# A hybrid mLSTM and attention step on one core: samples' output rows on 128 partitions, output weights loaded inside the heads' output product, third K tile's sums moved

## The chip, the cores and the metric

The kernel runs on one core of one Trainium2 chip. The core has a matrix engine (TensorE, PE in the profile, with its weight loads as PEld), a vector engine (VectorE, DVE), a scalar engine (ScalarE, ACT), GpSimd (POOL) and a queue engine (SyncE, SP) that issues nearly all transfers. Each engine works through its own instructions in order; semaphores make one wait for another. The metric is the device time of one execution in microseconds; lower is better.

## The reference, cut to what matters

One layer over 1024 prompt tokens and 32 sample tokens (8 sequences of 4), width 1024, all in float32: an mLSTM branch and a windowed attention branch, merged by gates, then an output product and two residual and norm steps.

```python
y_m, C, n, m = mlstm_branch(mq, mk, mv, mi, mf, mo, mz, C0, n0, m0, b_i, b_f, g_mn)
y_a = o.astype(x.dtype) * jax.nn.silu(az)
u = jax.nn.sigmoid(gm) * (y_m @ w_mo) + jax.nn.sigmoid(ga) * (y_a @ w_ao)
x = x + gate * (u @ w_o)            # gate: one row for the prompt, one per sample sequence
y = rmsnorm(x, g_final)             # for the prompt and for the samples
```

The change is in the last two lines: `u @ w_o` (called w_out in the kernel), the residual and the norm, for 1024 prompt rows and 32 sample rows.

## The kernel before

The large products are float32. Each operand is split into a high and a low part (`wh`/`wl`, `h`/`l`), and three matmuls (high by high, high by low, low by high) make one product. Products of 2 by 2 blocks are done with seven products instead of four times two, from sums and differences of the blocks; the names b11, b21, b22, t1 to t4 are the seven operands on the weights' side.

The work comes in this order: norm and conditioning of the tokens; gates and heads with their states (pairs of products 0 to 13 in `pairs`: heads, gates, two query gates, four head gates), with the attention units and the samples' work beside them; the attention's output product (tiles ax, ay, az, aw); the heads' output product `w_mo` (eight pieces d = 0 to 7, tile g_w_mo, whose sums tgw_mo complete `u`); and then the row stage, which is where most of the change lies.

*The row stage.* The prompt's rows are done as four row pairs i = 0 to 3 (`blocks_of_rows`), 2 by 128 rows each. A pair takes seven products of 128 by 512, each of four K tiles (KA = 0, 1, 4, 5) by three matmuls, so twelve matmuls. They run in the order 1, 5, 6, 2, 7, 3, 4 (in the last pair 3 before 7), into PSUM tiles that the profile calls foX (products 1 and 2), foZ (5), foW (6 and 3, on a copy of foX) and foY (7 and 4, on a copy of foW). Their weights are, in that order, b11, t1, t2, b21, t3, b22, t4. The row operands u0 to u3 are split two or three products ahead by `row_start()`: a cast to the high part on ScalarE (u0wh), the low part by a subtraction on VectorE (u0wl). Where a sum is needed first it is formed on VectorE, as `us` for product 5. After the products come adds to the residual x_prompt (tiles rows_l and rows_h), squares on ScalarE, the norm's small chain (fss, fv, fy, fw) and the scaled output y_p.

*The samples' rows.* The 32 sample rows stand in a group of small products (tile fo), four products at a time, one for each 32-column strip of the array: 32 rows by 512 columns, with K tiles kq to kq+3 in the four strips. Four such groups cover the two halves of the columns and the two halves of K. They stand after product 6 and after product 3 in rows 0 and 1. Their weights are plain w_out, loaded into four tiles (misc 1 and 7, parts of rows_l and rows_h) that each group reuses. The four strips are summed afterwards on VectorE (tile fo8s) with 32 partitions.

*The output weights.* The prompt's weights are w_out times the gate, in seven sums per K tile, each split in two (wosh, wosl). They are formed by `out_weights()` beside the heads. Tiles 0, 1 and 4 are stored to DRAM (woD) and loaded again by `weights_out(n)` after each piece d of the w_mo product; tile 5 stays in SBUF. The third tile (4) begins at the head gates and waits until the samples of all heads are done.

*What sets the order.* TensorE's order is the order in which the code is written; a planner (`Side`) hands out the side work by estimated TensorE time (`side.now`), and each `yield` names a lag until the next step. In the row stage VectorE and ScalarE follow the code as well; before it the scheduler may move their instructions. SP issues transfers in one queue; a transfer that must wait for its buffer holds up all that are behind it.

## Time and profile before

| what | value |
|---|---|
| median of 3 runs | 841.75 us (840.94 to 841.95) |
| the profiled execution's own time | 841.93 us |
| its span | 840.1 us |
| TensorE busy | 808.5 us, 96% |
| VectorE busy | 605.7 us, 72% |
| ScalarE busy | 417.8 us, 50% |
| mean bandwidth | 197 GB/s |

The profile is of one execution. In a timeline's row stand start, duration, engine, source line, operation, tiles written and read, form and count, and in brackets the idle time before it and what ended it. Most work has line 220, 261 or 275, those of the helpers, so tiles tell the place. An idle engine matters only where the engine that sets the end waits for it.

### The profile page before, as it was taken

The numbers are of one execution on the slowest core, as the hardware profiler recorded it, in microseconds if no ns is written. First come the engines' busy times: TensorE is split into PE (matmuls) and PEld (weight loads), VectorE is DVE, ScalarE is ACT, GpSimd is POOL, SyncE is SP. The second block draws the span as 40 slices with busy tenths as digits, with TensorE's granted clock in tenths as the row PEclk, the third lists the DMA queues.
The fourth block names the chain that finished last, engine by engine and source line by source line (L and its number), as shares of the span: only waits on it lengthen the run. The fifth ranks groups of instructions, "written<-read, shape, count | busy, mean of one in ns | idle before, by whom it ended". The sixth has DMA issues, their size and how long they took to land. (4 is left out here: it accounts for less than half of the span.)

```text
span 840.1 us, 15038 instructions
## 1 busy us (share of the span) xinstructions
PE 808.5 (96%) x5105; PEld 665.6 (79%) x5105; DVE 605.7 (72%) x1503; ACT 417.8 (50%) x1019; POOL 46.4 (6%) x111
## 2 busy tenths in 40 slices
PE   6999999999999999999999999999999999959996
PEld 3779797888788788888888888888886789937775
DVE  4889886646656546577576977897879977844887
ACT  5664365655465564556557554444456541124332
POOL 0120000000000001000001010000014010000000
PEclk9999999999999999999999999999999999989999
DMA  9994667446445324637737744646384899274422
GB/s 336 365 318 154 221 192 224 140 160 207 155 131 181 129 88 157 225 90 275 250 117 219 255 153 153 199 145 201 137 290 164 260 372 369 65 270 150 157 101 107
DMA packets 113025, 165.49 MB, mean 197 GB/s; under 512 B 21152, under 2 KB 55072, under 8 KB 112916
## 3 DMA queue, kind: packets, MB, share of 16 engines
q1 hardware_dynamic: 107300, 153.78, 55.5%
q10 hardware_dynamic: 4176, 6.56, 2.1%
q0 software_dynamic: 1472, 4.20, 1.3%
q8 instruction: 40, 0.66, 0.3%
q14 instruction: 37, 0.30, 0.1%
HBM read 115.51 MB, written 50.00 MB: 197 GB/s over the span
## 5 line engine op out<-in xcount | busy, mean ns | idle before, releaser
L220 ACT ACTIVATE p<-p,nmx 128x256 f32<-128x256 f32 (+1 forms) x64 | 31.0, 486 | 18.7 <-DVE nmx L220 18.3
L275 PE MATMUL g_aq<-h_h,wh_aq 128*128 128x384 f32 (+1 forms) x96 | 32.2, 336 | 0.0
L275 PE MATMUL g_aq<-h_h,wl_aq 128*128 128x384 f32 (+1 forms) x96 | 30.9, 322 | 0.0
L275 PE MATMUL g_aq<-h_l,wh_aq 128*128 128x384 f32 (+1 forms) x96 | 30.8, 321 | 0.0
L275 PE MATMUL g_w_mo<-ym_l,wh_w_mo 128*128 128x384 f32 (+1 forms) x96 | 30.8, 321 | 0.0
L275 PE MATMUL g_w_mo<-ym_h,wh_w_mo 128*128 128x384 f32 (+1 forms) x96 | 30.8, 321 | 0.0
L275 PE MATMUL g_w_mo<-ym_l,wl_w_mo 128*128 128x384 f32 (+1 forms) x96 | 30.8, 321 | 0.0
L220 DVE CUSTOM_DVE_ANT_0 p<-sc,cst,sink 128x256 f32<-128x256 f32 (+1 forms) x64 | 26.1, 463 | 5.3 <-PE sc L275 5.2
L220 ACT CAST wosh<-wor 128x512 fp32r<-128x512 f32 x24 | 14.9, 620 | 16.8 <-DVE wor L220 16.8
L275 PEld LDWEIGHTS g_aq<-h_h,wh_aq 128*128 128x128 f32 x96 | 18.0, 188 | 2.6 <-issue 1.5
L220 DVE TENSOR_TENSOR et<-et,S 128x384 f32<-128x384 f32 (+1 forms) x12 | 6.1, 509 | 19.1 <-PE S L275 16.4
L220 DVE SCALAR_TENSOR_TENSOR tgw_mo<-tgw_mo,g_w_mo 128x384 f32<-128x384 f32 (+1 forms) x24 | 12.4, 518 | 10.2 <-PE g_w_mo L275 9.6
L261 POOL DMA_DIRECT2D oD<-uqv x16 | 8.8, 552 | 184.3 <-ACT uqv L220 164.6
L275 PE MATMUL sc<-ukv,uqv 64*128 64x256 f32 (+1 forms) x128 | 18.0, 390 | 0.7 <-DMA ukv<-kD 0.7
L220 DVE TENSOR_TENSOR wosl<-wor,wosh 128x512 fp32r<-128x512 f32 x24 | 16.4, 685 | 2.8 <-ACT wosh L220 2.7
L275 PEld LDWEIGHTS g_w_mo<-ym_l,wh_w_mo 128*128 128x128 f32 x96 | 18.0, 188 | 0.0
L275 PEld LDWEIGHTS g_w_mo<-ym_h,wh_w_mo 128*128 128x128 f32 x96 | 18.0, 188 | 0.0
L275 PEld LDWEIGHTS g_aq<-h_l,wh_aq 128*128 128x128 f32 x96 | 18.0, 188 | 0.0
L275 PEld LDWEIGHTS g_w_mo<-ym_l,wl_w_mo 128*128 128x128 f32 x96 | 18.0, 188 | 0.0
L275 PEld LDWEIGHTS g_aq<-h_h,wl_aq 128*128 128x128 f32 x96 | 18.0, 188 | 0.0
L220 DVE COPY p<-pt 128x512 f32<-128x512 f32 (+1 forms) x16 | 10.5, 654 | 10.3 <-PE pt L280 10.3
L220 ACT ACTIVATE sq<-rows_h 128x512 f32<-128x512 f32 (+2 forms) x14 | 8.1, 579 | 19.0 <-issue 14.4
(2057 smaller groups left out, 2830.6 us busy)
## 6 DMA issues: line engine op xcount, KB each, us to landing
x<-xT SPq DMA_DIRECT2D x16, 256.0 KB
early_h<-w_ada SPq DMA_DIRECT2D x8, 512.0 KB
adar_ga<-w_ada SPq DMA_DIRECT2D x16, 256.0 KB
wr_ga<-w SPq DMA_DIRECT2D x16, 256.0 KB
wr_gm<-w SPq DMA_DIRECT2D x16, 256.0 KB
taD<-gt SPq DMA_DIRECT2D x16, 256.0 KB
tmD<-gt SPq DMA_DIRECT2D x16, 256.0 KB
wor<-w_out SPq DMA_DIRECT2D x16, 256.0 KB
```

Source lines behind the costliest of these rows:

```text
L220: ins = f(*args, **kw)
L261: ins = (eng or nc.sync).dma_start(out, in_)
L275: in_order(nc.tensor.matmul(out, lhsT, rhs, start=start, stop=stop, skip_group_check=more))
```

## The change

1. *Samples on 128 partitions.* The four strips now hold the four blocks of 256 output columns, 32 rows each, instead of four K tiles. A group is eight products of 32 by 256 (two K tiles) and the strips need no sum afterwards: gate, residual, square and scaling work on tiles of 128 by 256 (gs8, x8, y8, gf8). The squares of the four strips are added by four one-column products (fo8s) ahead of product 5 in the last row. The groups stand after product 3 in row 0, after 6 and 3 in row 1, and after 6 in row 2. The layouts of x_sample, y_s and of gsD (the samples' gates in DRAM) follow.
2. *Loads.* Two output weights each more are asked for after d = 5 to 7, and the rest in row 0, after the first w_out loads and x_prompt in the code; gsD, g_final (now once for the prompt, and in four pieces for the samples) and x_sample follow them in the code.
3. *Third K tile.* Its sums begin at product 5 of pair 11 and no longer wait for the samples; its lag is 2.2.
4. *Row order.* In rows 0 to 2 the adds of products 7 and 3 stand before the next split. Rows 4 and 5 of the output blocks are multiplied by g_final on VectorE first and then scaled on ScalarE.

```diff
@@ out_weights
-                    lag = 3.0
+                    lag = 2.2 if k == KA[2] else 3.0
-                while k == KA[2] and len(samples_done) < NH + 1:
-                    yield 0.5, ""
@@ hook
-            if n == len(pairs) - NH + 1 and not begun:
+            if (n, i) == (11, 5):
                 begun.append(4)
@@ heads' output product
-            weights_out((3, 3, 3, 2, 2, 1, 0, 0)[d])
-        weights_out(len(wo_parts))
+            weights_out((3, 3, 3, 2, 2, 2, 1, 1)[d])
...
-        gsb, gf = misc[0], misc[2]
-        dma(gf, a["g_final"].to_broadcast((128, D)), True)
-        S.activation(gf, gf, AF.Copy, scale=-1.0)
-        dma(gsb[:NS], gsD, True)
+        gf = misc[2]
+        gs8, gf8, x8, y8 = (misc[0][:, c:c + 256] for c in range(0, D, 256))
...
+        def weighted(xb, c):
+            V.tensor_tensor(xb[:, c], xb[:, c], gf[:, c], op=ALU.mult)
@@ sample_rows
+            def load(q):
+                for n, t in enumerate(raws):
+                    k = 2 * q + n // 2
+                    dma(t, a["w_out"][k * 128:(k + 1) * 128, HALF[n % 2]], q == 0)
+
+            def products(q):
+                for n in range(8):
+                    k, j = 2 * q + n // 4, n % 4
+                    mm(acc[32 * j:32 * j + 32], u(k, SEQ, NS), raws[n // 2][:, 256 * (j % 2):256 * (j % 2) + 256], start=(k == 0), stop=(k == KT - 1), share=4)
...
-                for j in (32, 64, 96):
-                    V.tensor_tensor(sums[f], acc[f][j:j + 32], sums[f], op=ALU.add)
-                V.tensor_tensor(sums[f], sums[f], gsb[:NS, HALF[f]], op=ALU.mult)
+            V.tensor_tensor(gs8, acc, gs8, op=ALU.mult)
+            V.tensor_tensor(x8, x8, gs8, op=ALU.add)
+            square(x8, sq8)
@@ rows
         rows8 = sample_rows()
+        next(rows8)
...
-            aside(0)
+            if not i:
+                weights_out(len(wo_parts))
+                dma(gs8, gsD)
+                dma(gf, a["g_final"].to_broadcast((128, D)))
+                S.activation(gf, gf, AF.Copy, scale=-1.0)
+                for j in range(4):
+                    dma(gf8[32 * j:32 * j + 32], a["g_final"][:, 256 * j:256 * j + 256].to_broadcast((32, 256)))
+                S.activation(gf8, gf8, AF.Copy, scale=-1.0)
+                dma(x8, a["x_sample"])
...
+            if i == 3:
+                sum8 = pb([128, 512], "fo8s")[:, :1]
+                for j in range(4):
+                    mm(sum8[32 * j:32 * j + 32], cst[:, C_S32:C_S32 + 32], sq8, start=True, stop=True, share=4)
...
-            aside(0, 1, 2)
+            aside(1, 2)
             for c in range(2) if i else ():
-                rows_out(2 * i - 2 + c, before[0][c], rs[:, c:c + 1])
+                rows_out(2 * i - 2 + c, before[0][c], rs[:, c:c + 1], V if nxt else None)
...
             if nxt:
+                seventh()
                 row_start()
-                seventh()
                 square(xb[1][:, hi], ss[:, 3:4])
+                first_row()
                 row_start()
-                first_row()
                 aside(0, 1, 2)
```

What stands where on the engines follows from the code and the scheduler. The first place is SP's queue up to the first w_out loads. Before, from the last t4 weights on (ahead of them stand the last tgw_mo from tmD and the other ten weights of t3, b22 and t4):

```order
L261 DMA wo_t4h<-woDt41h 128x512
L261 DMA wo_t4l<-woDt41l 128x512
L261 DMA wo_t4h<-woDt44h 128x512
L261 DMA wo_t4l<-woDt44l 128x512
L261 DMA rows_l_8763<-g_final 128x1024
L261 DMA rows_l_8763<-gsD 32x1024 x2
L261 DMA rows_l_8763<-x_prompt 128x1024
L261 DMA rows_h_8764<-x_prompt 128x1024
L261 DMA rows_l_8763<-w_out 128x512 x2
L261 DMA rows_h_8764<-w_out 128x512 x2
```

After, from the last tgw_mo on:

```order
L261 DMA tgw_mo_2_8613<-tmD_166 128x288
L261 DMA rows_l_8747<-gsD 128x256
L261 DMA rows_l_8747<-g_final 128x1024
L261 DMA wo_b22h<-woDb220h 128x512
L261 DMA wo_b22l<-woDb220l 128x512
L261 DMA rows_l_8747<-g_final 32x256 x4
L261 DMA rows_l_8747<-x_sample 128x256
L261 DMA wo_b22h<-woDb221h 128x512
L261 DMA wo_b22l<-woDb221l 128x512
L261 DMA rows_l_8747<-w_out 128x512 x2
L261 DMA rows_h_8748<-w_out 128x512 x2
L261 DMA rows_l_8747<-x_prompt 128x1024
```

The w_out loads moved ahead of x_prompt and of the last b22 and all t4 weights; gsD is now the first transfer behind tgw_mo, and x_prompt with those eight weights follows w_out.

The second place is VectorE at the end of the w_mo product, from the sum of its next to last part up to `us`, the operand of product 5 in row 0 (wosl, wor: the last K tile's weights). Before:

```order
L220 TENSOR_TENSOR wor_8204<-wor_8204,wor_8200 128x512
L220 SCALAR_TENSOR_TENSOR tgw_mo_1_8607<-tgw_mo_1_8607,g_w_mo_8705 128x384
L220 SCALAR_TENSOR_TENSOR tgw_mo_2_8609<-tgw_mo_2_8609,g_w_mo_8720 128x288
L220 TENSOR_TENSOR wosl<-wor_8204,wosh 128x512
L220 TENSOR_TENSOR us<-u_h_7686,u_l_7687 128x512
L220 TENSOR_TENSOR u_l_7687<-u_l_7687,tgw_mo_1_8607 128x384
```

After:

```order
L220 SCALAR_TENSOR_TENSOR tgw_mo_1_8611<-tgw_mo_1_8611,g_w_mo_8713 128x384
L220 SCALAR_TENSOR_TENSOR tgw_mo_2_8613<-tgw_mo_2_8613,g_w_mo_8728 128x288
L220 TENSOR_TENSOR wosl<-wor_8204,wosh 128x512
L220 TENSOR_TENSOR u_l_7687<-u_l_7687,tgw_mo_1_8611 128x384
L220 TENSOR_TENSOR wor_8204<-wor_8204,wor_8200 128x512
L220 TENSOR_TENSOR u_l_7687<-u_l_7687,tgw_mo_2_8613 128x288
L220 TENSOR_TENSOR wosl<-wor_8204,wosh 128x512
L220 TENSOR_TENSOR us<-u_h_7686,u_l_7687 128x512
L220 TENSOR_TENSOR u_h_7686<-u_h_7686 128x4x128
```

Between the last tgw_mo sum and `us` stood one wosl; now u_l's two adds, wor and a second wosl stand there too. The adds stood behind `us` before, wor and the other wosl ahead of the last two tgw_mo sums.

The third place is ScalarE in row 0, from the cast of `us` on (u0wh: high parts of the row operands; foW and foY: the copies that products 6 and 7 add to). Before:

```order
L220 CAST u0wh_8699<-us 128x512
L220 CAST u0wh_8769<-u_h_7686 128x512
L220 CAST u0wh_8784<-u_l_7687 128x512
L220 COPY foW<-foX 128x512
L220 CAST u0wh_8804<-u_h_7686 128x512
L220 CAST u0wh_8822<-u_l_7687 128x512
L220 COPY foY_8838<-foW 128x512
L220 CAST u0wh_8849<-u_l_7687 128x512
L220 ACTIVATE rows_l_8763<-rows_l_8763 128x1024
```

After:

```order
L220 CAST u0wh_8707<-us 128x512
L220 CAST u0wh_8754<-u_h_7686 128x512
L220 ACTIVATE rows_l_8747<-rows_l_8747 128x1024
L220 ACTIVATE rows_l_8747<-rows_l_8747 128x256
L220 CAST u0wh_8788<-u_l_7687 128x512
L220 COPY foW<-foX 128x512
L220 CAST u0wh_8808<-u_h_7686 128x512
L220 CAST u0wh_8826<-u_l_7687 128x512
L220 COPY foY_8842<-foW 128x512
```

The scaling of g_final (rows_l, 128 by 1024) moved from behind all casts to ahead of the cast of u_l and of foW's copy, and that of the samples' pieces (128 by 256) stands beside it.

## The prediction

> **What bounds the kernel now.** I read the page's head first, then who waited for whom on TensorE, then the last 100 us product by product.

> ```profile
> span 840.1 us, 15038 instructions
> PE fo L275 <- DMA rows_l<-w_out: 8.6, 1, 8.6
> PE foY L275 <- DVE rows_h L220: 1.9, 2, 1.7
> PE ay L275 <- DVE wl_ao0D L220: 1.1, 1, 1.1
> PE by L275 <- DVE hg1z L220: 1.1, 1, 1.1
> PE aw L275 <- ACT aw L220: 0.5, 1, 0.5
> ```

> These five are all that TensorE waits for after 500 us (total, times, longest). It is the bound everywhere else, so an edit counts only if it adds or removes a TensorE wait, or TensorE work. Around the largest wait (busy us of PE, PEld, DVE, ACT and POOL, then clock, DMA share, GB/s):

> ```profile
> 735.00:745.00 10.00, 9.41 (x42) 7.07 (x40) 6.89 (x12) 3.99 (x9) 0.00 (x0) 1.00 0.96 344
> 745.00:750.00 5.00, 0.00 (x0) 0.00 (x0) 0.00 (x0) 1.61 (x3) 0.00 (x0) 0.79 0.51 164
> 750.00:755.00 5.00, 1.95 (x5) 0.54 (x6) 2.58 (x4) 0.00 (x0) 0.00 (x0) 0.50 0.78 284
> 755.00:760.00 5.00, 5.00 (x16) 2.77 (x14) 0.00 (x0) 0.00 (x0) 0.00 (x0) 0.68 0.65 211
> ```

> After the wait the clock is at half, so the wait costs more than its 8.6 us. The TensorE rows of the row stage:

> ```profile
> 735.28 0.39 PE L275 MATMUL foX<-wo_b11h,u0wh 128*128 128x512 f32 x1
> ...
> 741.26 0.41 PE L275 MATMUL foW<-wo_t2h,u0wh 128*128 128x512 f32 x1
> ...
> 753.05 1.92 PE L275 MATMUL fo<-rows_l,u_h 128*32 128x512 f32 x3 [8.64 <-DMA rows_l<-w_out]
> ...
> 763.06 0.39 PE L275 MATMUL foW<-wo_b22h,u0wh 128*128 128x512 f32 x1
> ...
> 765.56 0.39 PE L275 MATMUL foW<-wosh,u0wl 128*128 128x512 f32 x1
> ...
> 766.87 0.50 PE L275 MATMUL foY<-wo_t4h,u0wh 128*128 128x512 f32 x1
> ...
> 769.73 0.39 PE L275 MATMUL foX<-wo_b11h,u1wh 128*128 128x512 f32 x1
> ...
> 809.69 0.47 PE L275 MATMUL foY<-wo_t4h,u2wh 128*128 128x512 f32 x1 [1.66 <-DVE rows_h L220]
> ...
> 812.50 0.39 PE L275 MATMUL foX<-wo_b11h,u3wh 128*128 128x512 f32 x1
> ```

> Row 0 runs from 735.28 to 769.73, 34.45 us; rows 0 to 2 together run to 812.50, 77.22 us. The twelve matmuls of foW start from 763.06 to 765.56: eleven steps of 0.227, so a product is 2.73 us and seven are 19.09. A samples' group at full clock lies between 765.56 + 0.23 and 766.87: 1.08 us.

> Why the weights are late is in the queue (SP) and on VectorE:

> ```profile
> 711.39 2.87 SPq L261 DMA_DIRECT2D tgw_mo<-tmD  x3
> 730.68 0.32 SPq L261 DMA_DIRECT2D wo_t3h<-woDt34h  x1
> ...
> 739.29 0.33 SPq L261 DMA_DIRECT2D rows_l<-g_final  x1
> ...
> 746.67 0.41 SPq L261 DMA_DIRECT2D rows_l<-x_prompt  x1
> ...
> 747.60 0.90 SPq L261 DMA_DIRECT2D rows_l<-w_out  x2
> ...
> 750.48 0.69 DVE L220 TENSOR_TENSOR rows_l<-rows_l,foZ 128x512 f32<-128x512 f32 x1 [7.72 <-DMA rows_l<-x_prompt]
> ```

> SP stands for 16 us, passes fourteen weight loads, g_final and gsD, and issues w_out at 747.60; the group can run at 753.05.

> **The rows, −15.2.** After the change w_out stands ahead of x_prompt and of the last eight weight loads, and row 0 has one samples' group instead of two, after product 3. Without waits rows 0 to 2 hold 3 × 19.09 = 57.27, two single opening matmuls of row 0 (2 × 0.23 = 0.45) and four groups (4 × 1.08 = 4.32): 62.04 instead of 77.22. That is −15.2, and holds three things: the 8.6 us wait, the slow matmuls after it, and the two foY waits of 1.9. Those two came from VectorE's add of product 7 standing behind a split that waits for ScalarE; in the new order the add comes first, so I remove them whole.

> Is w_out on time? SP now stands longer: its first load into the rows' tile waits for the last g_w_mo product, about 735.4, instead of 730.7. Behind that come, in MB summed up, gsD and g_final 0.66, the first b22 1.18, g_final's four pieces and x_sample 1.44, the second b22 1.97, w_out 3.01, x_prompt 4.06, the third b22 4.59, t4 6.16. At 344 GB/s that is 744.2 for w_out, 747.2 for x_prompt and 753.3 for t4. From issue to use x_prompt took 3.8 us (746.67 to 750.48), of which 1.5 is its own 0.52 MB, so 2.3 come on top: 746.5, 749.5, 755.6. The group is due at about 756, t4's last tile 2.5 later. Their cost is 0; they are the cover that a slower queue would use up (rivals).

> **A new wait at products 5 and 6, +3.7.** This is the part the change does not speak of.

> ```profile
> 735.48 0.46 DVE L220 SCALAR_TENSOR_TENSOR tgw_mo<-tgw_mo,g_w_mo 128x288 f32<-128x288 f32 x1 [0.64 <-PE g_w_mo L275]
> 735.85 0.68 DVE L220 TENSOR_TENSOR wosl<-wor,wosh 128x512 fp32r<-128x512 f32 x1
> 736.45 0.68 DVE L220 TENSOR_TENSOR us<-u_h,u_l 128x512 f32<-128x512 f32 x1
> 737.05 0.55 DVE L220 TENSOR_TENSOR u_l<-u_l,tgw_mo 128x384 f32<-128x384 f32 x1
> ...
> 737.22 0.62 ACT L220 CAST u0wh<-us 128x512 fp32r<-128x512 f32 x1 [2.20 <-DVE us L220]
> 739.49 0.62 ACT L220 CAST u0wh<-u_h 128x512 fp32r<-128x512 f32 x1 [1.65 <-DVE u_h L220]
> ...
> 740.54 0.57 ACT L220 COPY foW<-foX 128x512 f32<-128x512 f32 x1
> ...
> 746.18 1.06 ACT L220 ACTIVATE rows_l<-rows_l 128x1024 f32<-128x1024 f32 x1 [0.63 <-DMA rows_l<-g_final]
> ```

> VectorE forms `us`, the operand of product 5, with one instruction (wosl) between it and the sum that follows the last g_w_mo product. In the new order four more stand between: an add of 384 columns (about 0.5; row 737.05 is its kind), wor 0.60 (the step from 735.85 to 736.45), an add of 288 columns 0.37 (the step from 735.48 to 735.85), and a second wosl, 0.60, which first waits some 0.3 for ScalarE's cast (0.62) of that wor: 2.4. So `us` starts near 738.8 instead of 736.45, its cast 0.77 later (as 737.22 follows 736.45), and that ends near 740.2. Product 5 starts then instead of at 738.2: +2.1, and about +0.3 more at its third matmul, which needs the low half.

> ScalarE then has g_final ahead of the copy that product 6 adds to. The cast of u_h moves from 739.49 to about 741.9; g_final's scaling (1.06) and that of its pieces (about 0.3) follow, then a cast (0.53) and foW's copy (0.57), which ends near 744.9; product 5 would end at 743.6. Another +1.3: together +3.7. The pieces are issued eight places after 735.4, at 0.47 each (746.67 to 747.60 is two): 739.1, and landed by about 741.4 to 742.9; ScalarE is there at 743.4. Below: 2.2, if half of that finds gaps. Above: 5, if the pieces come 1.3 late.

> **The samples' groups, +0.8.** Eight products of 256 columns replace four of 512; the columns are the same. Between two halves the weights change once more. Loads of this kind:

> ```profile
> 765.87 0.11 PEld L275 LDWEIGHTS fo<-rows_l,u_h 128*32 128x32 f32 x2 [0.35 <-issue]
> ...
> 765.91 0.12 PEld L275 LDWEIGHTS fo<-rows_h,u_l 128*32 128x32 f32 x2
> ```

> Lower end 0 (all four overlap a matmul); upper end eight loads of 0.11 in a row per group, 4 × 0.88 = 3.5. I take two loads per group, 0.2, since here eight start within 0.04 us and so overlap each other: 0.8. [...] No run here shows a second load into a busy column group.

> Four one-column products of the samples' square sums in row 3 add 0.2 (an opener's 0.23); they wait for ScalarE's square of the samples, which I put at the same moment that TensorE gets there (bounds 0 and 1). VectorE's sums for the samples shrink, with nothing waiting for them. ScalarE takes over four scalings of rows 4 and 5 in row 3 (about 0.6 each by foW's copy, 2.4), ahead of the cast for the last product, which comes three products, 8.2 us, later. The order of the last 25 VectorE instructions is as before; I add 0.3 for row 3 and the tail together (bounds −0.3 and 1).

> **The third K tile, −1.8.** Fifteen VectorE instructions (0.60 steps, about 9.2 us), seven casts, six loads and fourteen stores move from about 590–625 to about 507–545.

> ```profile
> 505.00:550.00 45.00, 45.00 (x274) 36.55 (x274) 35.66 (x84) 21.10 (x45) 1.96 (x10) 1.00 0.52 166
> ...
> 593.00:625.00 32.00, 32.00 (x198) 26.39 (x197) 25.24 (x47) 16.39 (x32) 0.14 (x1) 1.00 0.65 214
> 625.00:660.00 35.00, 32.33 (x164) 24.19 (x163) 34.52 (x63) 21.44 (x47) 10.66 (x6) 1.00 0.68 221
> ...
> 549.06 0.68 DVE L220 TENSOR_TENSOR wl_phead_gate__6624<-wr_mo,wh_phead_gate__6623 128x512 fp32r<-128x512 f32 x1
> ...
> 555.44 0.39 PE L275 MATMUL bx<-h_h,wl_phead_gate__6624 128*128 128x512 f32 x1
> ```

> VectorE has 9.3 us idle in 505–550 (45.00 less 35.66) and gets 9.2: it will be full, and late by perhaps 3 us at the end. The tightest of the weight splits there is ready at 549.74 and used at 555.44, 5.7 us later, so that lateness is covered: 0. Without that cover it would be up to 3. Stores on SP now stand ahead of head loads and wait for VectorE; the same 5.7 us cover them.

> In 625–660 VectorE is busy 34.52 of 35, and there lie the three waits (1.1, 0.5, 1.1). With 9 us less just ahead, hg1z and the ao0D split stand two or three instructions of 0.60, some 1.5 us, earlier in VectorE's order. I take 1.8 of 2.7; bounds 0 and 2.7.

> **Sum.** −15.2 + 3.7 + 0.8 + 0.2 + 0.3 − 1.8 = −12.0, against the profiled execution's own 841.93 (span 840.1 and 1.8 around it; 0.2 over the median of 841.75): 829.9, told as 830.0. All low ends give about 826, all high ends about 838; a measurement of this kernel tells 0.2% from no change.

> **Rivals.**
> - *The clock drops again.* If TensorE's two new waits act like the old one, the clock is at half for about 8 us, as in 750–760 (0.50 and 0.68), some 4 us: 834. For it: both lie within 7 us. Against: the three waits in 625–660 left the clock at 1.00. [...] Chance 0.10.
> - *The narrow groups pay their weight loads one by one.* 3.5 instead of 0.8: 832.7. For it: no row shows a reload; against: the eight that start within 0.04 us. Chance 0.08. [...]
> - *VectorE overruns its cover at 545–560.* Up to 3 us: 833. Against: 5.7 us of cover. Chance 0.05.
> - *Slower: the bunched loads.* 6.16 MB stand behind one wait at 735.4. To eat 12 us, t4's last tile must land at about 770.5, so the queue would have to run below 6.16 / (770.5 − 735.4 − 2.3) = 188 GB/s; at 211, as in 755–760, t4 lands at 766.9, 8.4 late, with half a clock after it (some 2): 840.4. At 150 GB/s it lands at 778.8: about 852. Against: 344 GB/s in 735–745. Chance of slower than before 0.06; of a partial loss (833–841) 0.06.
> - *The change does not do what it says*: w_out still comes last because SP stays blocked, about 838. Against: it stands twelfth after 735.4, and 0.47 each makes 741. Chance 0.03.

> The forecast itself has 0.62. The range 826.5–835.0 leaves out the slower cases and the far ends. Faster by over 0.2%: 0.91; within: 0.02 and slower: 0.07, most of it from the bunched loads.

> **What would show it.** No TensorE wait for w_out, and clock 1.00 throughout 745–760; new TensorE waits near 738–741 (foZ, for ScalarE's cast of us) and near 743–745 (foW, for ScalarE); no wait at foY in rows 1 and 2; groups of eight between 1.1 and 1.5 us; nothing at 505–560; smaller waits at by and ay. Wrong if TensorE waits for b22 or t4, or if waits of over 1 us appear before 600.

## The result: 1.5% faster, and the profile after

The changed kernel takes 828.62 us (828.52 to 828.77), the kernel before in the same rounds 841.35 (840.49 to 841.95): a ratio of 0.985, with a 95% interval of 0.9833 to 0.9867, or 12.7 us less. In a second comparison it took 829.40 against 840.44, 0.987 (0.9857 to 0.9884), 11.0 us less. Predicted were 830.0.

The head of the changed kernel's page:

```profile
span 826.8 us, 15097 instructions
```

All that its TensorE waits for after 500 us (total, times, longest):

```profile
PE foZ L275 <- ACT u0wh L220: 1.9, 1, 1.9
PE bx L275 <- DVE zt L220: 1.2, 1, 1.2
```

The five waits of before (fo, foY, ay, by, aw; 13.2 us) are gone, and two new ones stand there, 3.2 us. One was predicted in place and size (foZ), the other (bx) was put at nothing.

Its row stage in TensorE's timeline (start, duration, operation, and in brackets the idle time before it), mostly the first matmuls of products and groups:

```profile
731.89 0.39 PE L275 MATMUL foX<-wo_b11h,u0wh 128*128 128x512 f32 x1
...
736.96 0.50 PE L275 MATMUL foZ<-wo_t1h,u0wh 128*128 128x512 f32 x1 [1.94 <-ACT u0wh L220]
...
741.66 0.40 PE L275 MATMUL foW<-wo_t2h,u0wh 128*128 128x512 f32 x1
...
752.59 0.39 PE L275 MATMUL foW<-wosh,u0wl 128*128 128x512 f32 x1
752.91 0.64 PE L275 MATMUL fo<-rows_l,u_h 128*32 128x256 f32 x8
...
753.91 0.50 PE L275 MATMUL foY<-wo_t4h,u0wh 128*128 128x512 f32 x1
...
756.80 0.39 PE L275 MATMUL foX<-wo_b11h,u1wh 128*128 128x512 f32 x1
...
798.68 0.39 PE L275 MATMUL foX<-wo_b11h,u3wh 128*128 128x512 f32 x1
```

Row 0 is 24.91 us long (34.45 before), rows 0 to 2 are 66.79 (77.22 before): 10.4 less; the prediction's terms for them gave 15.2 - 3.7 - 0.8 = 10.7. The group starts with no wait behind product 3 and takes 753.91 - 752.59 - 0.23 = 1.09.

By slices of time (busy us of PE, PEld, DVE, ACT, POOL, then granted clock, DMA share and GB/s), from the new wait to the place of the old stall:

```profile
735.00:737.00 2.00, 0.06 (x2) 0.04 (x1) 1.95 (x4) 0.62 (x1) 0.00 (x0) 1.00 0.97 323
737.00:739.00 2.00, 2.00 (x6) 1.33 (x7) 1.26 (x3) 0.68 (x2) 0.00 (x0) 0.76 0.87 271
739.00:741.00 2.00, 2.00 (x7) 1.52 (x6) 0.92 (x2) 2.00 (x4) 0.00 (x0) 0.50 0.78 253
741.00:743.00 2.00, 2.00 (x9) 1.64 (x8) 1.73 (x3) 1.36 (x3) 0.00 (x0) 0.89 0.91 299
...
745.00:750.00 5.00, 5.00 (x24) 4.14 (x23) 2.66 (x5) 0.96 (x2) 0.00 (x0) 1.00 1.03 386
750.00:755.00 5.00, 5.00 (x35) 3.44 (x34) 3.09 (x5) 2.44 (x6) 0.00 (x0) 1.00 0.50 173
```

From 745 on TensorE is never idle and the clock is full, where before it stood for 8.6 us and then ran at half. The transfers run at 386 GB/s in 745 to 750. Instead, just after the 1.94 us wait, the clock is at half from 738.0 to 741.4. In the queue's timeline (SP) w_out is issued at 738.51, where before it was 747.60, and x_prompt 6.4 earlier:

```profile
738.51 0.81 SPq L261 DMA_DIRECT2D rows_l<-w_out  x2
...
740.31 0.43 SPq L261 DMA_DIRECT2D rows_l<-x_prompt  x1
```

The order of the loads isn't all of this. In before gsD was asked for twice into the same tile, as the queue's order ahead of the prediction shows (x2), and SP held the second load until the first had landed. The two in SP's timeline of before:

```profile
739.91 6.70 SPq L261 DMA_DIRECT2D rows_l<-gsD  x2
```

In SP's own waits of before:

```profile
SPq L261 <- DMA rows_l<-gsD: 5.7, 1, 5.7
```

In these 5.7 us SP asked for nothing more, and at their end the transfers ran nearly dry (61 GB/s in 744 to 746, 86 in 746 to 748). The changed kernel asks for gsD once, and its SP has no such wait. Neither the prediction nor a run takes this apart from the order, so what the second load cost by itself stays open.

The timeline of VectorE and of ScalarE at the new wait (`us` is the operand of product 5):

```profile
733.53 0.69 DVE L220 TENSOR_TENSOR wor<-wor,wor 128x512 f32<-128x512 f32 x1
734.13 0.45 DVE L220 TENSOR_TENSOR u_l<-u_l,tgw_mo 128x288 f32<-128x288 f32 x1
734.90 0.69 DVE L220 TENSOR_TENSOR wosl<-wor,wosh 128x512 fp32r<-128x512 f32 x1 [0.32 <-ACT wosh L220]
735.51 0.69 DVE L220 TENSOR_TENSOR us<-u_h,u_l 128x512 f32<-128x512 f32 x1
...
736.29 0.62 ACT L220 CAST u0wh<-us 128x512 fp32r<-128x512 f32 x1 [1.42 <-DVE us L220]
...
738.84 1.36 ACT L220 ACTIVATE rows_l<-rows_l 128x1024 f32<-128x1024 f32 x2
740.11 0.60 ACT L220 CAST u0wh<-u_l 128x512 fp32r<-128x512 f32 x1
740.62 0.57 ACT L220 COPY foW<-foX 128x512 f32<-128x512 f32 x1
```

These are instructions that the prediction named: an add, wor and a second wosl ahead of `us`, with a wait of 0.32 for ScalarE's cast; then both scalings of g_final (1.36) ahead of the copy of foW.

Laid side by side by TensorE's start times, the two profiles differ by 13.3 us in span. 1.3 of it arises before 100 us, where nothing was changed: two waits for transfers, of 0.5 and 0.7, that the profile of before has there and the other has not. The rest is -2.0 between 500 and 670 (the K tile), +3.8 from there to the start of product 6 of row 0, and -13.7 behind that: -12.0 in all, rounded.

### The profile page after: what moved, and what is told of

It is laid out like the page before. It is cut to its first block, busy times and chain, and to the rows that moved or that the text cites. A ratio compares the mean times of both kernels' runs of the same rounds, so it can differ in the third digit from the quotient of the medians.

```text
span 826.8 us, 15097 instructions
## 1 busy us (share of the span) xinstructions
PE 805.8 (97%) x5145; PEld 667.2 (81%) x5145; DVE 598.7 (72%) x1495; ACT 418.5 (51%) x1020; POOL 46.6 (6%) x111
## 4 chain that ended last, share of the span: by engine, by line
PE 91%; DVE 4%; DMA 2%; ACT 1%; issue 1%; SPq 0%; ACTq 0%; DVEq 0%
PE bx L275 11%; PE bw L275 11%; PE by L275 11%; PE g_aq L275 6%; PE g_w_mo L275 6%; PE bz L275 5%; PE g_mq L275 3%; PE foW L275 3%; PE foY L275 2%; PE smp L275 2%; PE foX L275 2%; PE sc L275 2%; PE oT L275 2%; PE pt L280 2%; PE n L275 2%; PE foZ L275 2%
## 5 line engine op out<-in xcount | busy, mean ns | idle before, releaser
L220 ACT ACTIVATE p<-p,nmx 128x256 f32<-128x256 f32 (+1 forms) x64 | 31.1, 486 | 18.9 <-DVE nmx L220 18.4
L275 PE MATMUL g_aq<-h_h,wh_aq 128*128 128x384 f32 (+1 forms) x96 | 32.2, 336 | 0.0
L275 PE MATMUL g_aq<-h_h,wl_aq 128*128 128x384 f32 (+1 forms) x96 | 30.9, 322 | 0.0
L275 PE MATMUL g_aq<-h_l,wh_aq 128*128 128x384 f32 (+1 forms) x96 | 30.8, 321 | 0.0
L275 PE MATMUL g_w_mo<-ym_l,wh_w_mo 128*128 128x384 f32 (+1 forms) x96 | 30.8, 321 | 0.0
L275 PE MATMUL g_w_mo<-ym_h,wh_w_mo 128*128 128x384 f32 (+1 forms) x96 | 30.8, 321 | 0.0
L275 PE MATMUL g_w_mo<-ym_l,wl_w_mo 128*128 128x384 f32 (+1 forms) x96 | 30.8, 321 | 0.0
L220 DVE CUSTOM_DVE_ANT_0 p<-sc,cst,sink 128x256 f32<-128x256 f32 (+1 forms) x64 | 26.1, 463 | 5.3 <-PE sc L275 5.2
L220 ACT CAST wosh<-wor 128x512 fp32r<-128x512 f32 x24 | 14.9, 622 | 21.8 <-DVE wor L220 21.8
L220 DVE SCALAR_TENSOR_TENSOR tgw_mo<-tgw_mo,g_w_mo 128x384 f32<-128x384 f32 (+1 forms) x24 | 12.5, 519 | 11.2 <-PE g_w_mo L275 10.7
L275 PEld LDWEIGHTS g_aq<-h_h,wh_aq 128*128 128x128 f32 x96 | 18.0, 188 | 2.6 <-issue 1.5
L220 DVE TENSOR_TENSOR et<-et,S 128x384 f32<-128x384 f32 (+1 forms) x12 | 6.1, 510 | 19.3 <-PE S L275 16.5
L261 POOL DMA_DIRECT2D oD<-uqv x16 | 8.9, 558 | 183.6 <-ACT uqv L220 170.4
L220 DVE TENSOR_TENSOR wosl<-wor,wosh 128x512 fp32r<-128x512 f32 x24 | 16.5, 688 | 3.1 <-ACT wosh L220 3.0
L275 PEld LDWEIGHTS g_w_mo<-ym_l,wh_w_mo 128*128 128x128 f32 x96 | 18.0, 188 | 0.0
L275 PEld LDWEIGHTS g_aq<-h_l,wh_aq 128*128 128x128 f32 x96 | 18.1, 188 | 0.0
L275 PEld LDWEIGHTS g_w_mo<-ym_h,wh_w_mo 128*128 128x128 f32 x96 | 18.0, 188 | 0.0
L275 PE MATMUL sc<-ukv,uqv 64*128 64x256 f32 (+1 forms) x128 | 18.0, 390 | 0.0
L275 PEld LDWEIGHTS g_aq<-h_h,wl_aq 128*128 128x128 f32 x96 | 18.0, 188 | 0.0
L275 PEld LDWEIGHTS g_w_mo<-ym_l,wl_w_mo 128*128 128x128 f32 x96 | 18.0, 188 | 0.0
L220 DVE COPY p<-pt 128x512 f32<-128x512 f32 (+1 forms) x16 | 10.5, 656 | 10.3 <-PE pt L280 10.3
L275 PE MATMUL g_mq<-h_h,wh_mq 128*128 128x384 f32 (+1 forms) x48 | 16.8, 350 | 0.3 <-ACT mk L220 0.3
```

The lines of the kernel that those rows point to most:

```text
L220: ins = f(*args, **kw)
L261: ins = (eng or nc.sync).dma_start(out, in_)
L275: in_order(nc.tensor.matmul(out, lhsT, rhs, start=start, stop=stop, skip_group_check=more))
```

## The experiments

All differences are against the kernel before in the same rounds, whose median was 839.99 to 840.86. What was open: which part of the change takes the stall away, whether the parts add, what the slow clock after the new wait costs, and whether the new wait can be had back.

### The groups' place alone, the queue's order alone, and both

`b_groups_later`: the samples' groups one place later, the first behind product 3.

```diff
-            aside(0, 1, 2)
+            aside(1, 2)
             for c in range(2) if i else ():
...
                 aside(0, 1, 2)
+                aside(2)
                 row_start()
                 r.product(4, Y[0], False)
```

> The kernel before, with only the place of the samples' groups changed: the first stands behind product 3 of row 0 instead of behind product 6, and each later one takes the next place; the queue's order is left. Theory A (it is the groups' place alone that removes the stall): the first group is due three products (8.2 us) later, near 752.5, where w_out landed at 753.05, so 8.6 us of wait and the 3 to 4 us of slow matmuls after it go: 829 to 830. Theory B (the place in the queue is needed as well): x_prompt stands behind the same weight loads, VectorE's adds of foZ wait for it until about 750.5 and 752, and the split for product 3 stands behind them, so product 3 waits some 3 us and the clock falls once more: about 833. Rival: nothing gained, the stall only moves: 841.

Measured: 832.53 against 839.99, 0.9911 (0.9884 to 0.9938), -7.5. Theory B, with its number. TensorE's largest wait after 500 us in that kernel:

```profile
PE foW L275 <- DVE u0wl L220: 3.9, 1, 3.9
```

The split for product 3 stands on VectorE behind the adds of foZ, which wait for x_prompt; 3.9 us of TensorE's time and a half clock for 6.8 us are left of the old stall in the profiled execution. That one took 2.7 us more than the median and had a mean granted clock of 0.993; the other three had 0.996 to 0.998, so the half clock isn't the same in each.

`b_loads_first`: the last seven pairs of weight loads behind x_prompt and w_out.

```diff
-        weights_out(len(wo_parts))
...
             aside(0)
+            if not i:
+                weights_out(len(wo_parts))
             X, Z = pg([128, 512], "foX"), pa([128, 512], "foZ")
```

> The kernel before, with only the queue's order changed: the last seven pairs of weight loads stand behind x_prompt and the samples' first w_out tiles. The group stays behind product 6. Theory: w_out lands near 745 to 746.5, where the group is due at 744.0; 1 to 2.5 us of wait are left of 8.6, the clock holds, and the time is 841.4 - 12 + 2 = about 831 to 833. Rival: the later weight loads now come last and TensorE waits for them (b22, t4) by more than 2 us instead: 834 to 838.

Measured: 837.30 against 839.99, 0.9966 (0.9952 to 0.9981), -2.7: neither. The wait for w_out is nearly gone, as the theory said, but in TensorE's waits another stands in its place:

```profile
PE foZ L275 <- ACT u0wh L220: 2.6, 1, 2.6
...
PE fo L275 <- DMA rows_l<-w_out: 0.7, 1, 0.7
```

ScalarE's timeline in the same kernel:

```profile
739.28 1.06 ACT L220 ACTIVATE rows_l<-rows_l 128x1024 f32<-128x1024 f32 x1 [4.41 <-DMA rows_l<-g_final]
740.24 0.60 ACT L220 CAST u0wh<-us 128x512 fp32r<-128x512 f32 x1
```

With g_final issued early, its scaling moved ahead of the cast of `us` in ScalarE's order and waited 4.41 us for the transfer; the cast behind it came 3.0 later than in the profile of before (740.24, where 737.22 stood). The wait cost 2.6 and a half clock for 6.8 us. The second gsD load is still there too: the two issues took 4.35 us of SP's time (735.70 to 740.05), ahead of x_prompt and w_out.

`d_groups_loads`: both edits together, and the scaling of g_final behind the copy of foW.

```diff
-        S.activation(gf, gf, AF.Copy, scale=-1.0)
...
             W = copied(X, "foW", pg, new=r.w[1] if i == 0 else None)
+            if not i:
+                S.activation(gf, gf, AF.Copy, scale=-1.0)
```

> The kernel before with both of the places changed that were tried apart: the samples' groups stand later, and the last weight loads behind w_out and x_prompt; g_final's scaling stands behind the copy of foW, so that ScalarE doesn't wait for it ahead of product 5. The third K tile, the splits' order and the shape of the samples' rows are as before. Theory: neither place does it alone (7.5 and 2.7 us), both together take the whole stall of row 0: 34.45 - 21.7 = 12.7 us, so about 828 (ratio 0.985), with row 0 between 21.7 and 22.5 us long, and no wait over 1 us in it. Rival: the parts only add up: 840.4 - 10.2 = 830.2.

Measured: 832.67 against 840.86, 0.9908 (0.9894 to 0.9922), -8.2. Below both: the parts overlap instead of adding. Row 0 is 24.47 us long, with one group in it. Products 7 and 3 stand in pieces, in TensorE's timeline:

```profile
749.13 0.50 PE L275 MATMUL foY<-wo_t3h,u0wh 128*128 128x512 f32 x1 [0.74 <-DMA wo_t3h<-woDt34h]
...
749.80 0.50 PE L275 MATMUL foY<-wo_t3l,u0wh 128*128 128x512 f32 x1 [0.17 <-DMA wo_t3l<-woDt34l]
...
751.70 0.50 PE L275 MATMUL foW<-wo_b22l,u0wh 128*128 128x512 f32 x1 [0.18 <-DMA wo_b22l<-woDb220l]
```

By slices of time (columns as above) the transfers run at 374 to 388 GB/s all the while:

```profile
745.00:750.00 5.00, 4.09 (x17) 2.85 (x17) 3.13 (x5) 1.69 (x4) 0.00 (x0) 1.00 1.03 374
750.00:755.00 5.00, 4.47 (x15) 2.32 (x15) 2.94 (x5) 1.29 (x3) 0.00 (x0) 1.00 1.05 388
```

The two products take 4.19 and 4.70 us (746.87 to 751.06 to 755.76) instead of 2.73 each, 3.4 too much. Here the transfers are the bound, and t3 and b22 come late: the rival of the bunched loads in small. Two causes remain for it. Seven pairs stand behind x_prompt, where the changed kernel has four; and SP still holds the second gsD load ahead of all of them (SP's waits):

```profile
SPq L261 <- DMA rows_l<-gsD: 3.2, 1, 3.2
```

In 739 to 740 the queue moved nothing. These 3.2 us are nearly the 3.4 that the products lose, and no run parts the two.

`e_loads_late` was to price just those three pairs, on the fastest kernel (`d_us_late2`, below).

```diff
-            weights_out((3, 3, 3, 2, 2, 2, 1, 1)[d])
+            weights_out((3, 3, 3, 2, 2, 1, 0, 0)[d])
```

> The fastest kernel so far (the changed one with t4's last sum and g_final's scalings moved, 825.5, ratio 0.982) with one part of the change undone: the three pairs of weight loads that the change sets inside the last w_mo products stand behind x_prompt again, seven pairs there instead of four. Theory: the transfers are then the bound in 745 to 755, as in the run of both places apart from the rest, where products 7 and 3 of row 0 waited in five pieces for t3 and b22 at 374 to 388 GB/s and row 0 was 2.8 us longer than 21.7; so 2 to 3 us slower: 828, ratio 0.985. Rival: without the samples' early w_out load in the way the seven pairs still land in time: 825.5.

Measured: 839.36 against 840.01, 0.9986 (0.9977 to 0.9995), 14 us above the fastest. It doesn't answer its question. The scheduler set gsD and g_final behind all the weight loads, at 746.94 and 747.61, and ScalarE stood for the scaling, with the copy of foY behind it, for which TensorE waited 12.0 us. ScalarE's timeline:

```profile
753.62 1.06 ACT L220 ACTIVATE rows_l<-rows_l 128x1024 f32<-128x1024 f32 x1 [14.78 <-DMA rows_l<-g_final]
```

What the early loads are worth by themselves stays open; the 3.4 us at products 7 and 3 of the run before are the nearest that was measured, and they hold the second gsD load as well (the 2.8 of the expectation counted two groups into row 0, where one stands).

### The order of splits and adds

`b_row_order` is the kernel before with this part alone.

```diff
             if nxt:
+                seventh()
                 row_start()
-                seventh()
                 square(xb[1][:, hi], ss[:, 3:4])
-                row_start()
                 first_row()
+                row_start()
```

> The kernel before, with only the order of the splits and adds behind products 7 and 3 changed as in the new kernel (the add of product 7 ahead of the next split). Theory: the two foY waits in rows 1 and 2 go, 1.9 us: 839.5. Rival: TensorE waits somewhere else by as much, the split being later: 841.4.

Measured: 839.00 against 839.99, 0.999 (0.9979 to 1.0), -1.0, with an interval that reaches no change. Both foY waits go, and one of 1.14 comes in the last row, where VectorE's scaling of the samples' rows (1.40) stands ahead of the adds that product 4 waits for (timeline):

```profile
823.83 1.40 DVE L220 SCALAR_TENSOR_TENSOR rows_h<-rows_h,fy,rows_l 32x512 f32<-32x512 f32 x2
...
826.30 0.35 PE L275 MATMUL foY<-wo_t4h,u3wh 128*128 128x256 f32 x1 [1.14 <-DVE rows_h L220]
```

So of the 1.9 us some 1.1 come only with the other parts: the changed kernel scales the samples in one instruction of 128 by 256, and TensorE has no such wait there. The groups' later place does the same as this order: in `b_groups_later` and `d_groups_loads`, where the splits and adds stand as before, TensorE's waits show no foY wait for rows_h in rows 1 and 2 either, and one of 1.1 in the last row. Either part is enough for the two waits, and the runs don't say which of them the changed kernel owes it to.

### The third K tile

`b_ktile_only` is the kernel before with this part alone, `a_ktile_back` the changed kernel without it.

```diff
-                    lag = 3.0
+                    lag = 2.2 if k == KA[2] else 3.0
...
-                while k == KA[2] and len(samples_done) < NH + 1:
-                    yield 0.5, ""
...
-            if n == len(pairs) - NH + 1 and not begun:
+            if (n, i) == (11, 5):
```

> The kernel before, with only the third K tile's sums moved as in the change. Theory: the loss at 555 (a TensorE wait at bx of some 1.2 us for VectorE's zt) and the gain in 625-660 (2.5 to 3.7 us: no waits at by, aw and ay) give -2.2 us together, of which all reaches the end, since w_out's landing is set by SP's wait for the last w_mo product and moves with it. The prediction had 0 and -1.8. Rival: w_out's landing is set by something that doesn't move (the queue), the wait at fo grows by the 2.2 us, and the time stays: 0.

> The changed kernel with the third K tile's sums back at their old place. Theory: that part of the change is worth what TensorE's aligned start times say between the two profiles, a gain of 3.7 us over 625-660 less a loss of 1.5 at 555, so -2.2; without it 828.6 + 2.2 = 830.8, with no TensorE wait at bx near 555 and waits at by, aw and ay of 2.5 to 3 us in 625-660. The prediction's own number gives 828.6 + 1.8 = 830.4. Rival: most of the 2.2 is variation between two executions, as the 1.3 us that TensorE gains before 100 us, where nothing was changed, may be: 828.6 to 829.3.

Measured: alone 838.56 against 840.44, 0.9978 (0.9967 to 0.9988), -1.9; without it 830.88 against 839.99, 0.989 (0.9871 to 0.9909), where the whole change has 0.985 and 0.987 (1.7 to 3.4 us apart; the interval overlaps with that of the second comparison, and just not with that of the first). The waits at by, ay and aw are in the second and gone in the first; the wait at bx is in the first (0.7) and gone in the second. In the changed kernel's timeline it looks so:

```profile
552.25 0.69 DVE L220 TENSOR_TENSOR wl_phead_gate__6701<-wr_mo,wh_phead_gate__6700 128x512 fp32r<-128x512 f32 x1
...
553.66 0.90 DVE L220 TENSOR_TENSOR Cs<-Cs,sxb 128x387 f32<-128x387 f32 x2
554.47 0.68 DVE L220 SCALAR_TENSOR_TENSOR zt<-zt,bx 128x512 f32<-128x512 f32 x1
...
555.21 0.50 PE L275 MATMUL bx<-h_h,wh_phead_gate__6700 128*128 128x512 f32 x1 [1.23 <-DVE zt L220]
...
555.78 0.39 PE L275 MATMUL bx<-h_h,wl_phead_gate__6701 128*128 128x512 f32 x1
```

The weight split (552.25 to 552.94) is in time, though its cover is down from 5.7 us to under 3. What is late is VectorE's read of the accumulator bx (554.47), which the next product must write; VectorE is busy 40.49 of the 45 us before 550, where it was 35.66.

### The new wait, and what its slow clock costs

`after_again` is the changed kernel once more, beside `c_fill`, which puts eight surplus matmuls into the wait.

```diff
             row_start()
+            for _ in range(0 if i else 8):
+                mm(Z, r.w[1][0][:, 0], wo["b11"][KA[0]][0], start=True, stop=True)
             r.product(5, Z, True)
```

> The changed kernel itself once more, on the same chip and in the same rounds as the three below, since the kernel before was 1.4 us apart in the two comparisons so far (841.4 and 840.0). Expected 827.3 to 828.6, ratio 0.985. Its profile also tells which small waits vary between executions: if the waits of 0.5 to 0.7 us near 55 and 93 us that only the first profile of before shows are variation, they may be here or not.

> The changed kernel with eight more matmuls in row 0 between products 1 and 5, into the accumulator that product 5 then overwrites; they take 8 x 0.227 = 1.8 us of the 1.94 us in which TensorE waits for the cast of us. They are surplus work. Theory: the idle time of 1.9 to 2.1 us is what halves the clock from 738 to 741.4; without it foZ's twelve matmuls take 2.73 us instead of 4.4, so 1.7 us faster than the changed kernel (about 826), granted clock 1.00 in 737 to 743, and no new wait at foW of more than 0.5 (its copy ends at 741.2). Rival 1: the slow steps of foZ are its operands coming late (the low half of us, the weights t1), not the clock: same time as the changed kernel. Rival 2: the surplus work only takes the wait's place and ends later: up to 1 us slower.

Measured: 829.40 and 829.32 against 840.44, 0.987 (0.9857 to 0.9884) and 0.9869 (0.9853 to 0.9884): the filled wait gains nothing, and the theory falls. The time is rival 1's, but not for its reason: at full clock just one of foZ's operands is late, by 0.2 us. The second profile of the changed kernel says why. In its timeline the wait of 1.94 is the same, but the clock stays at 1.00 after it, and a second wait comes up, which the half clock had hidden:

```profile
738.25 0.50 PE L275 MATMUL foZ<-wo_t1h,u0wh 128*128 128x512 f32 x1 [1.94 <-ACT u0wh L220]
...
742.54 0.50 PE L275 MATMUL foW<-wo_t2h,u0wh 128*128 128x512 f32 x1 [0.99 <-ACT foW L220]
```

The slice of time in which the first profile has a clock of 0.50:

```profile
739.00:741.00 2.00, 2.00 (x9) 1.65 (x10) 1.21 (x2) 1.39 (x2) 0.00 (x0) 1.00 1.00 305
```

Product 6 can't start before ScalarE's copy of foW, whatever TensorE does until then. From the row's start to product 6 it is 9.36 us here (733.18 to 742.54), 9.35 with the surplus matmuls, 9.77 in the profile with the half clock: by these two profiles of one kernel the slow clock cost 0.4, not 1.7. In before it was 5.98, so the new wait costs 3.4 to 3.8.

The waits for transfers near 55 and 93 us differ from profile to profile (this one has 0.3 and 0.2 there, the kernel with the K tile alone 1.3 at the second): they are variation between executions.

### The wait taken away

`c_us_late` and `d_us_late2` move the two causes: the last sum and split of t4, and the scalings of g_final, behind the copy of foW.

```diff
+                if k == KA[-1]:
+                    tail.append((k, b21, b11))
+                    return
                 V.tensor_tensor(b21, b21, b11, op=ALU.subtract)
                 keep("t4", k, b21)
...
             W = copied(X, "foW", pg, new=r.w[1] if i == 0 else None)
+            if not i:
+                later[0]()
+                S.activation(gf, gf, AF.Copy, scale=-1.0)
+            if i == 1:
+                S.activation(gf8, gf8, AF.Copy, scale=-1.0)
```

(`later[0]()` does the two instructions left out above. In `c_us_late` both scalings stand in row 0.)

> The changed kernel with two moves: the sum and split of the last weight tile (t4, two instructions on VectorE and a cast) behind product 1 of row 0 instead of ahead of us, and ScalarE's two scalings of g_final behind the copy of foW. Theory: us starts near 733 instead of 735.5, its cast ends near 734.6 and product 5 starts on time near 735.0 + 0.2, so the wait of 1.94 and the slow clock after it (1.7) both go: 3 to 3.6 us faster than the changed kernel, 825 to 825.6 where that takes 828.6. Rival: the wait comes back at product 6 (foW's copy or the low half of u_h): half of it, 827; or the moved split makes t4 late for product 4: 828 or more.

> The changed kernel with t4's last sum and split behind product 1 and g_final's scaling behind the copy of foW, as in the run above, but the scaling of g_final's four pieces only in row 1, since in the run above those pieces had slid to the end of the queue and ScalarE waited 10.5 us for them. Theory: the wait for us and the wait for foW's copy both go and nothing takes their place: product 7 of row 0 starts 11.7 us after the row does, as in the run above (743.54 - 731.84), instead of 15.2, so 3.5 us faster than the changed kernel: ratio 0.983 to the kernel before, 825.9 where that has 840.4. Rival: another load has slid as well and TensorE waits for it: 828 or more.

Measured: `c_us_late` 837.76 against 840.44, 0.9968 (0.9956 to 0.9981), the rival and worse than it. Products 5 and 6 run without a wait, but three of the four pieces of g_final had slid to the end of the queue, and ScalarE waited for them, with the copy of foY behind it, for which TensorE stood 9.7 us. ScalarE's timeline:

```profile
751.47 0.42 ACT L220 ACTIVATE rows_l<-rows_l 128x256 f32<-128x256 f32 x1 [10.46 <-DMA rows_l<-g_final]
```

`d_us_late2` 825.50 against 840.86, 0.9818 (0.9804 to 0.9831), 15.4 us less: the fastest of all, ahead of the changed kernel's 0.985 and 0.987. TensorE's waits after 500 us are down to these, none in the rows:

```profile
PE bx L275 <- DVE zt L220: 1.4, 1, 1.4
PE aw L275 <- ACT aw L220: 0.2, 1, 0.2
```

Product 6 starts 5.98 us after the row (732.35 to 738.33), as in the kernel before. That is the term +3.7 had back, by moving instructions whose results nobody needs yet.

`d_us_ktile` also begins the third K tile one pair earlier (`(n, i) == (10, 5)`).

> The run above, with the third K tile's sums begun one pair of products earlier, so that they lie near 487 to 525, where VectorE is 6 to 8 of 10 us busy, instead of 508 to 545. Theory: the wait of 0.8 to 1.2 us at bx near 555 goes: 1.0 us faster than the run above (about 825). Rival: VectorE is short there too and a wait of the same size appears before 540: same time; or worse, the samples' attention on VectorE is held up: 1 us slower.

Measured: 826.56 against 840.86, 0.983 (0.9817 to 0.9844): 1.1 slower than `d_us_late2`. The rival: the wait at bx goes, and two others come, the first near 489 (TensorE's waits after 300 us):

```profile
PE ty L280 <- ACT smps L220: 1.7, 1, 1.7
PE smp L275 <- ACT gts L220: 0.4, 1, 0.4
```

## Why the prediction was right, by its steps

The forecast was -12.0, to 830.0; the comparisons gave -12.7 and -11.0, and the two profiles -13.3, of which 1.3 has no part in the change. That leaves -12.0, the forecast itself. In part this is luck: the gain of the rows was put 1.0 too high and the cost of the groups 0.8 too high, and the two nearly cancel.

- *The rows, -15.2: right in kind, 1.0 too much.* Without the new wait of 3.8 rows 0 to 2 take 63.0 us, where 62.04 was counted. The group behind product 3 waits for nothing and the clock holds from 745 on. w_out landed in time and the weights too: no wait for b22 or t4. x_prompt came 14.7 us after the queue went on (732.08 to 746.78), where 14.1 was estimated (735.4 to 749.5): from 735 to 745 the queue ran at 253 to 333 GB/s in slices of 2 us, not at 344. That neither the queue's order nor the groups' place does it alone was not argued in the prediction and is shown by the runs: -7.5 and -2.7. What was misread is the queue: the 16 us were the first of two stands, and the second, of 5.7 us for the doubled gsD load, went as well without being priced.
- *The foY waits: right, for a reason only half given.* They are gone, but the order alone would have lost 1.1 of 1.9 again in the last row, to VectorE's scaling of the samples, which another part of the change makes shorter; and the groups' later place takes the same two waits away without the order.
- *The new wait, +3.7: right in place, cause and size.* 1.94 us at foZ behind the four instructions named, and 0.99 at foW behind g_final's scaling; 3.4 to 3.8 in all, within the bounds of 2.2 and 5. In one of the two profiles the half clock stands where the foW wait would be.
- *The samples' groups, +0.8: too much.* A group of eight takes 1.09, as four of 512 columns did (1.08); the term is 0. The rival that charged all eight weight loads, 0.88 a group, falls: the reloads of a strip that is in use cost no time that the rows show. The kernel before had rows that spoke against it already, in the prompt's products: in row 0 a weight load of 0.19 us (128 by 128) starts together with the matmul ahead of it (both at 765.33), and the matmul that uses it starts 0.23 later (765.56).
- *fo8s and the tail, +0.5: right.* Row 3 and the end are 28.1 us long, 0.4 more than before; the four one-column products take 0.42 (801.18 + 0.23 to 801.83).
- *The third K tile, -1.8: right sum, wrong terms.* It was 0 at 505-560 and -1.8 of 2.7 at 625-660. The trace gives +1.7 and -3.7, the part alone -1.9 (-1.0 to -2.8). The step that failed is the cover: the 5.7 us were those of the weight splits, but the first thing to be late was the read of an accumulator on the same engine, which has no such lead. The rival "VectorE overruns its cover" named the place and went by the wrong instruction. And the relief was held too small: the waits at by, ay and aw gave their 2.7, and another 1.0 came in steps too small for the list of waits.
- *The clock drops again (0.10):* it did in one of two profiles, and cost 0.4 instead of 4, because TensorE would have waited for ScalarE in that time anyway.

## What to carry to other kernels

Price a stall by what is late next: two moves that each take away the same 8.6 us wait gave 7.5 and 2.7 alone and 8.2 together, since behind the one stood a split, behind the other a scaling that waited for its transfer, and behind both together loads that came late. When a transfer is moved in a queue, follow the instruction that waits for it and what is queued behind that on its engine: in three of these kernels TensorE stood 2.6 to 12.0 us because of a scaling of g_final that is used in row 1 at the earliest, and moving it, with two other instructions that were not yet needed, behind the urgent copy brought another 2.7 to 4.4 us beside the 11.0 to 12.7 of the change. Cover that was counted on weights, which are made ahead (5.7 us), didn't hold for the accumulator bx, which the next product writes again (1.2 us of wait).

## What the hardware showed

*The clock after a short idle time.* TensorE stood for 1.94 us in three profiles at the same place. In two of them the granted clock fell to half about 3.0 and 3.6 us after the wait had begun, when TensorE had been busy again for 1.1 and 1.7 us, and in one it didn't fall. Between the first products and the last, the waits of up to 1.67 us in these runs' profiles (that one in `d_us_ktile`, at 489.59) didn't do it, and the seven of 2.65 and more did. The slow stretches, read from the granted clock in slices of half a microsecond, have four lengths:

| TensorE idle for | kernel | clock at half | for |
|---|---|---|---|
| 1.94 | after | 738.0 to 741.4 | 3.4 |
| 1.94 | a_ktile_back | 742.0 to 745.4 | 3.4 |
| 1.94 | after_again | never | 0 |
| 2.65 | b_loads_first | 740.3 to 747.1 | 6.8 |
| 3.85 | b_groups_later | 753.2 to 760.0 | 6.8 |
| 7.34 | b_row_order | 748.4 to 755.2 | 6.8 |
| 7.36 | b_ktile_only | 745.0 to 755.2 | 10.2 |
| 8.64 | before | 747.9 to 758.2 | 10.2 |
| 9.74 | c_us_late | 747.1 to 757.3 | 10.2 |
| 12.03 | e_loads_late | 748.4 to 762.1 | 13.7 |

For the other profiles an estimate, with the same step of 3.41 counted back and on from the start of their slow stretches: the wait of 1.94 in a_ktile_back had 1.73 ahead of the edge at which the clock fell. The wait of 2.65 in b_loads_first ran on for 0.63 behind such an edge, in a stretch at half, and the next stretch was at half too. Idle times of 7.34 and 7.36 gave two and three: the one in b_row_order had 0.68 ahead of its first edge (744.94), where the clock stayed full, and the one in b_ktile_only 2.44 (744.97), where it fell. In after_again, where the clock is 0.98 over 765 to 825, an edge would lie inside the wait, with at most 1.6 us of idle time on either side. By these rows the price of a wait depended on where the edges fell as well as on how long it was. (Idle time is counted from the profile, in which the ends of matmuls are modelled.)

*Bandwidth.* Where loads stood back to back the queue moved 374 and 388 GB/s in slices of 5 us in `d_groups_loads` (745 to 755), and 386 in the changed kernel (745 to 750), above the 344 from which the landings had been estimated; between 735 and 745 it was 253 to 333 in the changed kernel, and why it was less there is open.
